# First two transfers moved ahead of the register moves, and SyncE's wait on the store moved into the closing block, in a streaming sum of absolute differences

## The chip, the cores and the metric

One core of one Trainium2 chip. Times are device microseconds of one execution of the program; the kernel before ran at 86.15 us (median of 6 runs beside the changed kernel). All runs told of here were in the fast state with a granted clock of 1.0. Profiles give a span, from the program's first record to its last; the time is 1.78 us longer than the span in nearly all runs (one exception is told below). Lines of the profile name VectorE DVE, ScalarE ACT, GpSimd POOL and SyncE SP; a q after the name means the engine's sequencer.

## The reference

```python
def reference(x, y, axis):          # x, y: 1024 x 4096 float32, axis -1
    return np.sum(np.abs(x - y), axis=axis).astype(np.float32)
```

33.55 MB go in, 4 KB come out.

## The kernel before

Rows lie on the 128 partitions, eight to each. SP loads x and the last four rows of y; ACT loads the first four rows of y. DVE subtracts, ACT takes the absolute value and sums along the row, the last row goes in four pieces that get smaller, and SP stores the eight sums of each partition. All waits are written by hand. The helper `put` takes an instruction just emitted and moves it into the program's first block: either ahead of the engine's opening drain, which is the start of the barrier that opens the program, or ahead of its branch out of that block.

```python
    def put(self, emit, early=False):
        ...
        before = "Drain" if early else "UnconditionalBranch"
        while len(here) > n:
            mine = here.pop(n)
            first = next(i for i, x in enumerate(main) if x.engine == mine.engine and x.opcode == before)
            main.insert(first, mine)
```

```python
    put(lambda: nc.sync.dma_start(out=xa, in_=xr[:, 0:H, :]).then_inc(s_first, 16), early=True)
    put(lambda: nc.scalar.dma_start(out=yb, in_=yr[:, 0:H, :]).then_inc(s_first, 16), early=True)
    put(lambda: nc.sync.dma_start(out=xb[:, 0:H - 1, :], in_=xr[:, H:K - 1, :]).then_inc(s_xb, 16))
    # ... (other loads, subtractions, sums)
    put(lambda: nc.sync.wait_ge(s_end, n_part + 3))
    put(lambda: nc.sync.dma_start(out=orr, in_=ro).then_inc(s_out, 16))
    put(lambda: nc.sync.wait_ge(s_out, 16))
```

The last line waits until the sums are in HBM. Behind it comes the closing block, which the framework writes: a barrier of all engines, GpSimd clearing the semaphores, a second barrier.

## Time and profile before

| | us |
|---|---|
| time, median (range) of 6 runs | 86.15 (85.93 to 86.25) |
| span of the profiled run | 84.33 |
| first issue to first data packet | 1.00 |
| first packet to last load's landing | 79.63 |
| last landing to the store's issue | 1.36 |
| store's issue to its landing | 1.41 |
| store's landing to the end | 0.93 |

The five rows below the span add up to it. The second of them is a stream at 421 GB/s and holds 94% of the span. The change moves no byte, so its effect is to be looked for in the other four, 4.7 us in all. The profile's lines for this are in the prediction below.

### The profile page before, as it was taken

How to read it: one execution, taken by the hardware profiler on the slowest of the kernel's cores; microseconds unless marked ns; L12 is line 12 of the kernel's file. 1: busy time of each engine (PE TensorE's matmuls, PEld its weight loads, DVE VectorE, ACT ScalarE, POOL GpSimd, SP SyncE). 2: the span in 40 equal slices, each digit the busy share in tenths (PEclk: the TensorE clock that was granted, in tenths of full speed). 3: DMA queues.
4: the chain of work that ended last, by engine and by line, in shares of the span. 5: the costliest groups of instructions: out<-in, count | busy, mean ns of one | idle time of the engine just before them, and what ended most of it. 6: DMA issues, size and time to landing. Idle time of an engine off the chain costs nothing.

```text
span 84.3 us, 98 instructions
## 1 busy us (share of the span) xinstructions
DVE 36.5 (43%) x15; ACT 31.2 (37%) x25; POOL 0.2 (0%) x4
## 2 busy tenths in 40 slices
DVE  0000000000000000000399999999199897988870
ACT  5000000000000000000002979797970967999950
POOL 0000000000000000000000000000000000000000
DMA  9199999983999999749999888899999999999900
GB/s 497 62 435 497 497 497 497 497 373 155 466 497 497 497 497 497 342 187 466 396 606 490 373 373 373 381 427 427 420 443 412 451 404 414 425 397 404 341 0 2
DMA packets 2160, 33.56 MB, mean 398 GB/s; under 512 B 368, under 2 KB 624, under 8 KB 1392
## 3 DMA queue, kind: packets, MB, share of 16 engines
q1 hardware_dynamic: 2016, 25.17, 70.9%
q10 hardware_dynamic: 144, 8.39, 23.0%
HBM read 33.55 MB, written 0.00 MB: 398 GB/s over the span
## 4 chain that ended last, share of the span: by engine, by line
DMA 67%; DVE 16%; ACT 13%; ACTq 1%; issue 0%
DMA yb_rows<-in_y_dram 67%; ACT xb_rows L110 13%; DVE xa_rows L105 10%; DVE xb_rows L105 5%; ACTq L176 1%; DVE ro_sums L140 1%
## 5 line engine op out<-in xcount | busy, mean ns | idle before, releaser
L105 DVE TENSOR_TENSOR xa_rows<-xa_rows,yb_rows 128x4096 f32<-128x4096 f32 x4 | 17.4, 4421 | 41.5 <-DMA yb_rows<-in_y_dram 41.5
L110 ACT ACTIVATE xa_rows<-xa_rows 128x4096 f32<-128x4096 f32 x4 | 14.5, 3617 | 45.6 <-DVE xa_rows L105 45.6
L105 DVE TENSOR_TENSOR xb_rows<-xb_rows,yb_rows 128x4096 f32<-128x4096 f32 (+5 forms) x8 | 17.8, 2241 | 3.5 <-DMA yb_rows<-in_y_dram 3.4
L110 ACT ACTIVATE xb_rows<-xb_rows 128x4096 f32<-128x4096 f32 (+5 forms) x8 | 14.9, 1859 | 3.7 <-DVE xb_rows L105 3.7
L110 ACT ACT_TABLE_LOAD x1 | 1.3, 1283 | 0.9 <-PEq L162 0.9
L110 ACT ACTIVATION_READ_ACCUMULATOR xb_rows<-xb_rows 128x1 f32 x8 | 1.5, 188 | 0.0
L110 ACT ACTIVATION_READ_ACCUMULATOR xa_rows<-xa_rows 128x1 f32 x4 | 0.7, 186 | 0.0
L140 DVE TENSOR_REDUCE ro_sums<-last_piece 128x1 f32<-128x387 f32 x1 | 0.6, 556 | 0.2 <-ACT xb_rows L110 0.2
L138 DVE TENSOR_TENSOR last_piece<-xb_rows,yb_rows 128x384 f32<-128x384 f32 x1 | 0.6, 557 | 0.2 <-DMA yb_rows<-in_y_dram 0.2
L132 DVE TENSOR_REDUCE ro_sums<-part_sums 128x1 f32<-128x3 f32 x1 | 0.2, 156 | 0.2 <-ACT xb_rows L110 0.2
L162 POOL MEMSET const-bfloat16-1.0<- 128x1 bf16 x1 | 0.1, 102 | 0.0
L162 POOL MEMSET const-uint8-127<- 128x1 uint8 x1 | 0.1, 102 | 0.0
L162 POOL MEMSET const-float32-0.0<- 128x1 f32 x1 | 0.1, 99 | 0.2 <-issue 0.2
L162 POOL MEMSET const-float32-1.0<- 128x1 f32 x1 | 0.1, 99 | 0.0
## 6 DMA issues: line engine op xcount, KB each, us to landing
xb_rows<-in_x_dram SPq DMA_DIRECT2D x1, 6144.0 KB, 54.9
yb_rows<-in_y_dram SPq DMA_DIRECT2D x3, 2048.0 KB, 15.3
xb_rows<-in_x_dram SPq DMA_DIRECT2D x1, 992.0 KB, 17.9
yb_rows<-in_y_dram SPq DMA_DIRECT2D x1, 992.0 KB, 16.4
xb_rows<-in_x_dram SPq DMA_DIRECT2D x1, 544.0 KB, 17.4
yb_rows<-in_y_dram SPq DMA_DIRECT2D x1, 544.0 KB, 18.2
xb_rows<-in_x_dram SPq DMA_DIRECT2D x1, 320.0 KB, 18.6
yb_rows<-in_y_dram SPq DMA_DIRECT2D x1, 320.0 KB, 18.9
```

Source lines behind the costliest of these rows:

```text
L105: put(lambda: nc.vector.tensor_sub(out=tx, in0=tx, in1=ty).then_inc(s_sub, 1))
L110: put(lambda: nc.scalar.activation(tx, tx, ABS, accum_out=to).then_inc(sem, 1))
L132: put(lambda: nc.vector.reduce_sum(out=ro[:, K - 2:K - 1], in_=part6, axis=AX).then_inc(s_end, 1))
L138: put(lambda: nc.vector.tensor_sub(out=last[:, n_part:n_part + w], in0=tx, in1=ty).then_inc(s_end, 1))
L140: put(lambda: nc.vector.reduce_sum(out=ro[:, K - 1:K], in_=last, axis=AX, apply_absolute_value=True).then_inc(s_end, 1))
L162: nc = _bacc.Bacc("TRN2", target_bir_lowering=False, num_devices=1)
L176: with _tile.TileContext(nc) as tc:
```

## The change

Its intent: put the first x and y issues still earlier, ahead of the register moves that the framework puts at the head of each engine's program; and let SP wait for the store not in the branch that leads to the closing block, but behind it, at the block's head.

```diff
-    def put(self, emit, early=False):
+    def put(self, emit, before="UnconditionalBranch"):
 ...
-        before = "Drain" if early else "UnconditionalBranch"
 ...
+    def at_end(self, emit):
 ...
+        def closing(ins):
+            if done or nc.cur_bb.bb.name == here or ins.engine != mybir.EngineType.SP:
+                return
+            done.append(ins)
+            emit()
 ...
-    put(lambda: nc.sync.dma_start(out=xa, ...).then_inc(s_first, 16), early=True)
-    put(lambda: nc.scalar.dma_start(out=yb, ...).then_inc(s_first, 16), early=True)
+    put(lambda: nc.sync.dma_start(out=xa, ...).then_inc(s_first, 16), before="RegisterMove")
+    put(lambda: nc.scalar.dma_start(out=yb, ...).then_inc(s_first, 16), before="RegisterMove")
 ...
-    put(lambda: nc.sync.wait_ge(s_out, 16))
+    entry.at_end(lambda: nc.sync.wait_ge(s_out, 16))
```

`closing` is called for each instruction ahead of its being added; at SP's first one in the closing block it emits the wait, which so comes to stand in front of it. When the program is finished, a wait that stands alone is folded into the instruction behind it, where it can be: in the kernel before into SP's branch, in the changed one into SP's first closing drain.

More of the change, by code (lines that the diff above doesn't have):

```diff
@@ L44, in put @@
             main.insert(first, mine)
+    def at_end(self, emit):
+        nc = self.nc
+        hook = nc.inst_callbacks[-1]
+        here = nc.cur_bb.bb.name
+        done = []
+        def closing(ins):
[3 more added lines that the diff above has]
+            emit()
+        nc.remove_inst_callback(hook)
+        nc.push_inst_callback(closing)
+        nc.push_inst_callback(hook)
 @with_exitstack
@@ L59 @@
     H = K // 2
-    put = Entry(nc).put
+    entry = Entry(nc)
+    put = entry.put
     def sbuf(name, shape):
@@ L81 @@
     s_out = tc.alloc_semaphore("s_out")
-    put(lambda: nc.sync.dma_start(out=xa, in_=xr[:, 0:H, :]).then_inc(s_first, 16), early=True)
-    put(lambda: nc.scalar.dma_start(out=yb, in_=yr[:, 0:H, :]).then_inc(s_first, 16), early=True)
+    put(lambda: nc.sync.dma_start(out=xa, in_=xr[:, 0:H, :]).then_inc(s_first, 16), before="RegisterMove")
+    put(lambda: nc.scalar.dma_start(out=yb, in_=yr[:, 0:H, :]).then_inc(s_first, 16), before="RegisterMove")
     put(lambda: nc.sync.dma_start(out=xb[:, 0:H - 1, :], in_=xr[:, H:K - 1, :]).then_inc(s_xb, 16))
```

## The prediction

> **What bounds the kernel now.** I read the page of the profile first, then the listing of the first and the last microseconds in order of time, then the records of the two lines that hold the program's opening (L162) and closing (L176), then SyncE's own waits.
>
> From the page:
>
> ```profile
> span 84.3 us, 98 instructions
> DVE 36.5 (43%) x15; ACT 31.2 (37%) x25; POOL 0.2 (0%) x4
> DMA  9199999983999999749999888899999999999900
> HBM read 33.55 MB, written 0.00 MB: 398 GB/s over the span
> DMA 67%; DVE 16%; ACT 13%; ACTq 1%; issue 0%
> ```
>
> The DMA row is at 7 or more in all but three of its first 38 slices of 2.1 us, and a low digit has a neighbour that makes up for it (packets of 64 KB are counted where they start). DVE and ACT are under half busy. The kernel is a stream of 33.55 MB from HBM: the trace's first data packet starts at 1.00 us and the last load lands at 80.63 us, so 33.55 MB / 79.63 us = 421 GB/s. That stretch is 79.6 of 84.3 us; neither part of the change touches a byte of it. What can be moved is the 1.0 us ahead of it and the 3.7 us behind it.
>
> The opening, in order of time (start, duration):
>
> ```profile
> 0.00 0.38 SPq L84 DMA_DIRECT2D xa_rows<-in_x_dram  x1
> 0.12 0.36 ACTq L85 DMA_DIRECT2D yb_rows<-in_y_dram  x1
> ...
> 0.91 1.28 ACT L110 ACT_TABLE_LOAD   x1 [0.91 <-PEq L162]
> 0.91 0.33 SPq L86 DMA_DIRECT2D xb_rows<-in_x_dram  x1
> ```
>
> The span starts with SP's issue of x: there is no earlier record of the program on any engine. The listing of L162, which holds whatever the program does before the kernel's own lines, shows what SP and ACT do besides:
>
> ```profile
> L162 DVEq DRAIN  x1: 10/10/10, 0.1 to 0.1; - x1
> ...
> L162 SPq DRAIN  x1: 131/131/131, 0.4 to 0.4; - x1
> L162 ACTq DRAIN  x1: 145/145/145, 0.5 to 0.5; - x1
> ...
> L162 SPq EVENT_SEMAPHORE  x1: 17/17/17, 0.8 to 0.8; - x1
> L162 ACTq EVENT_SEMAPHORE  x1: 17/17/17, 0.8 to 0.8; - x1
> ```
>
> The reader is to see what is missing: one drain and one semaphore wait each, and no register move. The source creates five on each engine (a zero and four bounds), but nothing reads them; in the finished program of this kernel, which I built and listed, they have been dropped, and the x issue is already SP's first instruction and the y issue ACT's.
>
> The end, in order of time, then the records of L176 and SP's own waits:
>
> ```profile
> 80.66 0.56 DVE L138 TENSOR_TENSOR last_piece<-xb_rows,yb_rows 128x384 f32<-128x384 f32 x1 [0.15 <-DMA yb_rows<-in_y_dram]
> 81.41 0.56 DVE L140 TENSOR_REDUCE ro_sums<-last_piece 128x1 f32<-128x387 f32 x1 [0.19 <-ACT xb_rows L110]
> 81.99 0.35 SPq L144 DMA_DIRECT2D out_dram<-ro_sums  x1
> ```
>
> ```profile
> L176 SPq DRAIN  x3: 7/7/7, 83.6 to 83.9; - x3
> L176 SPq COMPARE_BRANCH  x1: 32/32/32, 83.4 to 83.4; - x1
> ```
>
> ```profile
> SPq L176 <- DMA out_dram<-ro_sums: 1.1, 1, 1.1
> SPq L176 <- PEq L176: 0.6, 2, 0.4
> ```
>
> The last load lands at 80.63; subtraction and reduction end at 81.96; the store is issued at 81.99 and has landed at 83.40 (1.4 us from issue to landing on the page of issues). SP waits for it, and the instruction that waits is its branch into the closing block: the wait has been folded into it, so it is recorded as COMPARE_BRANCH. No other engine has a branch record on L176. Then two all-engine barriers run, and the last record ends at 84.33. The trace's own records, finer than the 0.1 us of this view, give SP's steps: store's last increment 83.396, COMPARE_BRANCH 83.413, DRAIN 83.564, DRAIN 83.629, GpSimd's collecting wait 83.662, release 83.740, SP released 83.782, second barrier until 84.33.
>
> **What the Trainium skill says.** "Advanced Engine Details and Errata", section Control Flow Timing, gives a compare-and-branch about 108 ns and an unconditional branch about 51 ns. The trace has 32 ns for the branch's own record, but 151 ns from its start to the start of the next instruction, where a drain takes 65 ns to the next one; I use the 151. "Perfetto Trace Analysis", section on the sequencer-only instruction, says that the recorded window opens when the semaphores are satisfied, so waiting is not in it. The trace agrees: the branch's record opens 17 ns after the store's last increment, though SP had been at it since 82.34. "VectorE: DVE Perf Modes", section "The DRAIN you can't avoid", tells boilerplate drains of about 12 ns from pipeline flushes; SP's closing drains are of that kind at 7 ns. "DMA: Bandwidth & Descriptors", section Latency and other measured facts, has about 600 ns to the first byte of a transfer issued from SP or ACT: here SP's first issue ends at 0.38 and the first packet starts at 1.00, which is 0.62 us. That is latency of the transfer itself and no reordering of SP's instructions shortens it.
>
> **The change part by part.**
>
> *The first two issues ahead of the register moves.* It takes five register moves per engine from in front of SP's and ACT's first issues. In the finished program there are none in front: 0 moves x anything = 0. The DRAIN and barrier after the issues stay. Gain 0.00 us at the front. If putting the transfers first made moves survive behind them, SP would run at most six small instructions between the issue and its first drain. From the 65 ns between two closing drains I estimate 6 x 65 ns = 0.4 us of delay for the opening barrier, so the second x issue would go from 0.91 to 1.3 us. That lies beside the first 16.8 MB, whose landing DVE awaits until 41.45 us; the queues don't run dry before then. ACT's table load of 1.28 us has until 45.91 us. Cost on the path: 0.00 us.
>
> *The wait on the store at the head of the closing block.* The number of waits doesn't change: the last increment of the store still lets SP go. What changes is which instruction wakes. Before: wake in COMPARE_BRANCH, 151 ns to the first drain, 65 ns to the second, 33 ns to the collecting wait. After: the branch waits for nothing and is done (or disappears, as on the other engines) at about 82.34 to 82.5, under the store's flight of 1.4 us. The wait then stands in front of SP's first closing drain, and I expect it to be folded into that drain as other waits have been folded into the instruction behind them. So: wake in the drain (17 ns after the increment, at 83.413), 65 ns to the second drain (83.478), 33 ns to the collecting wait (83.511 rather than 83.662). Saved: 83.564 - 83.413 = 0.151 us. If it is not folded, a semaphore wait by itself wakes first; SP's own one at 83.782 is followed by a drain at 83.873, 91 ns later, and the saving is 0.151 - 0.091 = 0.06 us. All this is on the path that sets the end: SP is the last of the engines at the first closing barrier (ACT's and DVE's drains end at 81.41 and 82.01), and the rest follows the collecting wait unchanged.
>
> Sum: 0.00 + 0.15 = 0.15 us, so the span goes from 84.33 to about 84.18. Time and span of the profiled run differ by 86.11 - 84.33 = 1.78 us, which neither part touches: 84.18 + 1.78 = 85.96. From the median of the runs, 86.2 - 0.15 = 86.05. I take 86.0 between them: -0.2%.
>
> **The rivals.**
>
> 1. *The moves are real and were in the way, unrecorded ahead of the span.* For it: measured time is 1.78 us longer than the span, so something runs outside the records. Against it: the drains and memsets of the same source line are recorded, moves aren't, and the finished program has none. If true, five moves at an estimated 65 ns would give 0.3 us more at the front, and the time about 85.7. It would show in the time, but not in the span.
> 2. *The wait that replaces the branch costs as much.* A drain with a wait could be as slow to go on as the branch: the opening drains took 131 and 145 ns, against 7 at the close. For it: exactly those were behind a fresh DMA issue, and the new one follows the store's issue. Against: there they came right after the issue, here the store's 1.4 us lie between, and today's first closing drain is also behind that store and takes 7 ns. If true, nothing is saved: 86.15.
> 3. *An earlier start of the stream speeds up or disturbs the loads.* Only if the first issue moved at all; and at 421 GB/s throughout, a shift by a few tenths shifts the landings by no more.
>
> **Range and chances.** The three runs of the kernel before lie between 85.93 and 86.25, a spread of 0.32 us, twice the effect. The range of 85.75 to 86.3 holds the 0.06 to 0.15 us cases, the first rival's 85.7 nearly, and the run-to-run spread. Two per cent is 1.7 us: the whole stretch from the last landing to the end is 3.7 us, of which the change touches 0.15, so faster has 0.01, slower 0.01, within 2% 0.98.
>
> **What would show it.** Right: first records unchanged (x issue at 0.00, y at 0.12, second x at 0.91, first drain of SP behind the x issue); no COMPARE_BRANCH on SP; a drain within 20 ns of the store's last increment, the second 65 ns later; from the store's last increment to the end 0.93 us before, 0.78 after. Wrong in the first part: move records, or a second x issue later than 0.91. Wrong in the second: a gap of 0.1 us or more between wake and second drain. The whole would be wrong if the time fell by over 0.4 us, or if the stretch up to the last landing moved by more than the runs' own spread.

## The result, and the profile after

86.01 us (median of 6 runs, 85.85 to 86.10) against 86.15; ratio 0.9986, 95% interval 0.9969 to 1.0003. A ratio is the mean time of one kernel's fast runs over that of the other's fast runs of the same rounds, so not quite the ratio of the medians. By itself this interval doesn't exclude 1; a second, longer measurement on another occasion (22 runs against 26) gave 0.9979, from 0.9970 to 0.9989:

> The changed kernel itself once more, beside the next run on the same chip, because its first ratio (0.9986, interval 0.9969 to 1.0003) rests on six executions and doesn't exclude 1. My theory (0.155 us shorter closing): ratio 0.998, interval clear of 1. Rival (no gain in the time, only in the records): 1.000.

So the change gains some two thousandths, and that is clear of the spread: the means differ by 0.18 us here and by 0.15 us in 22 further runs of the same finished program (the second part alone, below); in the first six runs it was 0.12 us. For the 2% question it is the same time.

Where it comes from is in the records. The same lines of the page as before, then the opening in order of time (start, duration):

```profile
span 84.1 us, 97 instructions
DVE 36.5 (43%) x15; ACT 31.2 (37%) x25; POOL 0.2 (0%) x4
...
HBM read 33.55 MB, written 0.00 MB: 399 GB/s over the span
...
DMA 67%; DVE 16%; ACT 13%; ACTq 1%; issue 0%
```

```profile
0.00 0.38 SPq L101 DMA_DIRECT2D xa_rows<-in_x_dram  x1
0.12 0.36 ACTq L102 DMA_DIRECT2D yb_rows<-in_y_dram  x1
...
0.91 1.28 ACT L127 ACT_TABLE_LOAD   x1 [0.91 <-PEq L179]
0.91 0.33 SPq L103 DMA_DIRECT2D xb_rows<-in_x_dram  x1
```

Busy times, bytes and the shares of the chain that ended last stand still. The opening is what it was, to the hundredth of a microsecond; 97 records instead of 98. The missing one shows in the listing of the closing line (L193 here, L176 before; name, count, duration in ns min/median/max, start of the first and of the last in us):

```profile
L193 SPq DRAIN  x3: 7/7/7, 83.4 to 83.7; - x3
```

and in SP's own waits:

```profile
SPq L193 <- DMA out_dram<-ro_sums: 1.1, 1, 1.1
SPq L193 <- PEq L193: 0.6, 2, 0.4
```

There is no COMPARE_BRANCH on SP any more, and the first of SP's three closing drains starts at 83.4 where it started at 83.6. The waits are the same two, as long as before: 1.1 us for the store, 0.6 us in the barriers. What was taken out lay between them. The trace's records to the nanosecond, in us of each span:

| | before | after |
|---|---|---|
| last load landed | 80.633 | 80.587 |
| store's last increment | 83.396 | 83.347 |
| SP wakes, in | 83.413 COMPARE_BRANCH | 83.364 DRAIN |
| SP's next drain | 83.564 | none between |
| SP's barrier drain | 83.629 | 83.425 |
| GpSimd's collecting wait | 83.662 | 83.457 |
| GpSimd's drain ahead of the clearing | 83.821 | 83.616 |
| end | 84.329 | 84.125 |
| from the store's last increment to the end | 0.933 | 0.778 |

The closing is 0.155 us shorter. The spans differ by 0.204 us; the other 0.049 us had been gained by the time the store landed, of which 0.046 at the last load. No part of the change reaches there, and one of the runs below, whose program is that of the kernel before, has its last load at 80.747: this is spread of the stream.

### The profile page after: what moved, and what is told of

It reads as the page before. It is cut to its first block, busy times and chain, and to the rows that moved or that the text cites. A ratio compares the mean times of both kernels' runs of the same rounds, so it can differ in the third digit from the quotient of the medians.

```text
span 84.1 us, 97 instructions
## 1 busy us (share of the span) xinstructions
DVE 36.5 (43%) x15; ACT 31.2 (37%) x25; POOL 0.2 (0%) x4
## 4 chain that ended last, share of the span: by engine, by line
DMA 67%; DVE 16%; ACT 13%; ACTq 1%; issue 0%
DMA yb_rows<-in_y_dram 67%; ACT xb_rows L127 13%; DVE xa_rows L122 10%; DVE xb_rows L122 5%; ACTq L193 1%; DVE ro_sums L157 1%
```

## The experiments

My theory: the first part changes nothing in the finished program, and the second gains by taking one instruction, the branch with its wait, out of the path from the store's landing to the barrier. The rivals: the moves do run, unseen, ahead of the span; or the gain hangs only on the branch being out of the way and not on which instruction carries the wait; or there is no gain but spread.

**The first part alone.** Before it ran I compared the two finished programs, engine by engine and instruction by instruction with all operands and waits (names and line numbers aside): 22 instructions on SP, 21 on ACT, 23 on DVE, 17 on GpSimd, 7 on TensorE, all the same as in the kernel before. So this run is also a measure of what two measurements of one program differ by.

```diff
-    entry.at_end(lambda: nc.sync.wait_ge(s_out, 16))      # from the changed kernel
+    put(lambda: nc.sync.wait_ge(s_out, 16))
```

> Only the first part of the change: the first x and y issues are put ahead of the register moves; the wait on the store stays in SP's branch. The finished programs of this kernel and of the kernel before are the same on all five engines, instruction by instruction. My theory (the moves are dropped when the program is finished, so the part is empty): ratio 1.000 within 0.002, no move in the records, second x issue at 0.91 us, 0.93 us from the store's last increment to the end, a COMPARE_BRANCH of 32 ns on SP. Rival (the moves run ahead of the span, unrecorded): some 0.3 us less in the time at an unchanged span, ratio 0.9965.

Ratio 0.9997 (0.9986 to 1.0007; 22 runs against 51). SP's COMPARE_BRANCH is back, and 0.934 us pass from the store's last increment to the end. The listing of its closing line:

```profile
L193 SPq COMPARE_BRANCH  x1: 33/33/33, 83.5 to 83.5; - x1
```

The rival's 0.9965 is outside the interval. The part is empty.

**The second part alone.** Its finished program is in turn the same as that of the whole change.

```diff
-    ... .then_inc(s_first, 16), before="RegisterMove")    # both first issues
+    ... .then_inc(s_first, 16), before="Drain")
```

> Only the second part: SP's wait on the store at the head of the closing block, the first issues where they were. My theory (all of the gain is the branch's 151 ns becoming a drain's 61 to 65 ns and a drain less of distance): 0.78 us from the store's last increment to the end, no COMPARE_BRANCH, ratio about 0.998 (0.15 of 86.1 us). Rival (the gain came with the first part, or was no gain but spread): 0.93 us or ratio 1.000.

Ratio 0.9979 (0.9969 to 0.9989; 22 runs against 51), 0.778 us from last increment to end. All of the gain is here.

**A wait that stands alone.** A second wait, on sums that were ready long before, takes the place in the first drain, so that the wait on the store stays an instruction by itself:

```diff
-    entry.at_end(lambda: nc.sync.wait_ge(s_out, 16))
+    def twice():
+        nc.sync.wait_ge(s_end, n_part + 3)
+        nc.sync.wait_ge(s_out, 16)
+
+    entry.at_end(twice)
```

> The changed kernel with a second, long satisfied wait (on the sums) at the head of the closing block, so that the wait on the store stays an instruction by itself and the drain behind it carries the other. My theory (the saving hangs on the wait being folded into the first drain; a wait that stands alone is followed by its drain 91 ns later): SP wakes in an EVENT_SEMAPHORE, 91 ns to the first drain, 61 to the second, so 0.87 us from the store's last increment to the end, ratio about 0.999. Rival (what saves is only that the branch is out of the way, whatever carries the wait): 0.78 us.

SP wakes in an EVENT_SEMAPHORE (the record of a semaphore wait that stands alone) at 83.550, drains at 83.610 and 83.675: 60 ns and 65 ns, and 0.842 us from last increment (83.533) to end (84.375). The wait's record, and SP's waits in this stretch:

```profile
L164 SPq EVENT_SEMAPHORE  x1: 17/17/17, 83.5 to 83.5; - x1
```

```profile
SPq L164 <- DMA out_dram<-ro_sums: 1.1, 1, 1.1
SPq L197 <- PEq L197: 0.6, 2, 0.4
```

So the instruction that carries the wait matters, as my theory has it: 0.842 lies between 0.778 (folded) and 0.933 (branch). But the size I gave it, 91 ns, was too large: 60 ns. I had read it off SP's wait in the barrier. That one also counts its semaphore down, and the drain behind it waits for the same semaphore to be zero; which of the two makes it longer no run shows. The time says nothing here: ratio 0.9994 (0.9973 to 1.0014; 14 runs against 51).

**The wait given to GpSimd.** If the closing is a chain, what stands in it matters only behind the store's landing. SP's wait puts the whole first barrier behind it. But the store need only have landed when GpSimd clears the semaphores; so GpSimd waits, behind the first barrier, and the barrier runs while the store is in flight. (The cut leaves out `at_end`'s edit: it now takes the engine and which of its drains in the closing block.)

```diff
-    entry.at_end(lambda: nc.sync.wait_ge(s_out, 16))
+    entry.at_end(lambda: nc.gpsimd.wait_ge(s_out, 16), mybir.EngineType.Pool, 1)   # at GpSimd's second drain there
```

> The wait on the store is taken from SP altogether and given to GpSimd, folded into its drain ahead of the clearing of the semaphores, behind the first closing barrier. SP arrives at that barrier while the store is still in flight. My theory (the whole first closing barrier, 83.41 to 83.82 in the kernel before, is on the path only because SP waits ahead of it): GpSimd's drain ends the wait 17 ns after the store's last increment, then 0.51 us as before from that drain to the end: 0.53 us from last increment to end, 0.40 us less than before and 0.25 less than the change, ratio about 0.995 to before. Rival (the closing barriers cost the same wherever the wait stands, or the store lands later when the engines run on): 0.78 us or more, ratio 0.998.

Ratio 0.9934 (0.9913 to 0.9955; 6 runs), median 85.64 us. To read it, first GpSimd's records on the closing line of the kernel before, then those of this one:

```profile
L176 POOLq EVENT_SEMAPHORE  x4: 17/17/17, 83.7 to 84.2; - x4
L176 POOLq EVENT_SEMAPHORE_RANGE_CLEAR  x1: 113/113/113, 83.9 to 83.9; - x1
```

```profile
L196 POOLq EVENT_SEMAPHORE  x4: 17/17/17, 82.5 to 83.8; - x4
L196 SPq DRAIN  x3: 7/7/123, 82.3 to 82.7; - x3
L196 POOLq EVENT_SEMAPHORE_RANGE_CLEAR  x1: 113/113/113, 83.5 to 83.5; - x1
```

GpSimd's first collecting wait is now at 82.5, 0.8 us ahead of the store's landing (83.324), where it was 0.27 us behind it. GpSimd's drain, which carries the wait, starts at 83.348, and the end is at 83.856: 0.532 us from last increment to end, 0.40 less than before. SP waits no longer for the store:

```profile
SPq L196 <- PEq L196: 1.2, 2, 1.1
```

Its first drain took 123 ns instead of 7: it now comes 56 ns behind the end of the store's issue. That is hidden too. The run was repeated, because 0.9934 is more than 0.40 us explain:

> The kernel with GpSimd waiting for the store once more; its first ratio, 0.9934 from six executions, is 0.002 below what the 0.40 us of its trace explain (0.9953). My theory (only the closing shrinks): 0.9953, interval including it, 0.53 us from last increment to end, store 1.41 us from issue to landing. Rival (something more is gained that the closing doesn't show): 0.9934 again.

0.9943 (0.9922 to 0.9963; 6 runs against 26), median 85.66 us, 0.533 us from last increment to end and 1.419 us for the store. The interval holds the 0.9953 of the theory, and so did the first. Both means are some 0.5 us below that of before, though, 0.1 us more than the closing shows. In the two traces the rest lies ahead of the store, where this edit doesn't reach: the last load lands at 80.569 and 80.496, 0.064 and 0.137 us earlier than in the trace of before. With 6 runs each I leave open whether that is spread. This kernel beats both: correct, and 0.3 us under the changed one (means of 85.67 and 85.98 us on the same occasion).

**What a part at the front would have been worth.** The first part was empty; whether the front is on the path at all is another question. Drains stay in the finished program, so they can stand where the moves would have stood. All three kernels of this set have the changed closing.

```diff
+    for _ in range(24):
+        put(lambda: nc.sync.drain(), before="RegisterMove")
+    for _ in range(24):
+        put(lambda: nc.scalar.drain(), before="RegisterMove")
     put(lambda: nc.sync.dma_start(out=xa, ...
```

> The changed kernel with 24 drains ahead of the first issue on SP and on ACT: instructions that do stay in the program, where the dropped moves would have stood. Theory (what stands ahead of both first issues is on the path in full, so the first part of the change gained nothing only because there was nothing to pass): about 24 x 61 to 65 ns = 1.5 us later first packet, last load and end, ratio about 1.016 to before (1.5 less the 0.15 of the closing). Rival (a few instructions at the front are hidden by the transfers' latency of 0.6 us or by the stream): first packet at most 0.9 us later, ratio under 1.010.

Ratio 1.0098 (1.0084 to 1.0112; 4 runs against 41). The expected 1.5 us were wrong in size. The opening in order of time:

```profile
0.93 0.38 ACTq L106 DMA_DIRECT2D yb_rows<-in_y_dram  x1
1.25 0.36 SPq L105 DMA_DIRECT2D xa_rows<-in_x_dram  x1
```

24 drains cost SP 1.25 us, 52 ns each, and ACT 0.93 - 0.12 = 0.81 us, 33 to 34 ns each: less than the 61 to 65 ns between SP's closing drains. And the first data packet, at 1.941 us, is now y's: it follows the earlier of the two issues by 1.008 us. The number of the rival (under 1.010) came true, but not what it says: nothing was hidden by the latency, since issue to packet is 1.0 us as before, and the packet is 0.94 us later. The stream then takes 79.55 us, the last load lands at 81.491, and the closing is the changed kernel's 0.778. The time grew by a little more than the span; time less span is 1.95 us in this kernel instead of 1.78, and what makes up that 0.17 us no record shows. It stays open.

If the earlier issue counts, then delaying SP's alone must cost next to nothing:

```diff
+    for _ in range(24):
+        put(lambda: nc.sync.drain(), before="RegisterMove")
     put(lambda: nc.sync.dma_start(out=xa, ...
```

> The same 24 drains ahead of SP's first issue alone; ACT's y issue stays at the front. Theory (the stream is of both queues and only its first packet counts, since the first subtraction awaits both transfers): y's packets start at about 1.1 us in place of x's, the last load is 0.1 to 0.2 us later than without the drains, ratio about 1.000 to before. Rival (SP's queue has more than its share of the bytes, 25 of 33.6 MB, and its delay comes out at the end): 1.5 us later, ratio 1.016.

```profile
0.13 0.38 ACTq L104 DMA_DIRECT2D yb_rows<-in_y_dram  x1
1.25 0.37 SPq L103 DMA_DIRECT2D xa_rows<-in_x_dram  x1
2.02 1.28 ACT L129 ACT_TABLE_LOAD   x1 [2.02 <-PEq L181]
2.02 0.33 SPq L105 DMA_DIRECT2D xb_rows<-in_x_dram  x1
```

SP's first issue is 1.25 us late, yet the first packet (y's) comes at 1.146, 0.15 us later than before, and the last load lands at 80.779, 0.15 us later than before. The last load alone would prove little, since it came at 80.747 in a kernel without drains; but the ratio is 0.9996 (0.9989 to 1.0003; 21 runs against 41), which fits 0.15 us lost at the front and 0.155 gained at the close. The stream is one, whichever queue's packets begin it: 1.25 us of delay in one queue's start became 0.15 us. The second x issue, 1.1 us later than before, and ACT's table load, as late, cost nothing on top.

Last, six drains ahead of both, as many as the source has instructions there that are dropped (the five register moves and one more):

```diff
+    for _ in range(6):   # and the same for nc.scalar
+        put(lambda: nc.sync.drain(), before="RegisterMove")
```

> Six drains ahead of both first issues, the number of instructions that the source has ahead of SP's and of ACT's first issue and that are dropped from the finished program. Theory: 6 x 61 to 65 ns = 0.37 to 0.39 us later first packet and end; against the kernel before 0.38 - 0.15 = 0.23 us more, ratio about 1.0025. So much the first part would have been worth. Rival: under the spread, ratio 0.998 as the change itself.

```profile
0.32 0.38 SPq L105 DMA_DIRECT2D xa_rows<-in_x_dram  x1
0.34 0.39 ACTq L106 DMA_DIRECT2D yb_rows<-in_y_dram  x1
```

SP's issue moved by 0.317 us, the first packet from 0.999 to 1.321, the ratio is 1.0015 (1.0009 to 1.0022; 21 runs against 41). The expected 1.0025 lies outside the interval: it was worked out with 61 to 65 ns a drain, and here they cost 52. From 0.32 us at the front less 0.155 at the close I get 0.17 us, or 1.0019, which lies inside. So the front is on the path one for one, within the interval, and passing six instructions of a drain's kind would have been worth 0.32 us, twice what the second part gained. There was nothing to pass.

Over all of these kernels the stretch from the first packet to the last load's landing is 79.5 to 79.8 us, whichever queue began it.

## Why the prediction was right

It was right in the time (86.0 predicted, 86.01 measured), and the steps that carry it were:

- *First two issues: 0.00 us.* Right, and for the reason given: the finished programs are the same (first run), and the opening's records stood still in the changed kernel.
- *Wait in the closing block: 0.151 us.* Right: 0.155 in the records, 0.778 us from last increment to end where 0.78 was named. The wait was folded into the first drain, SP woke 17 ns after the increment, and the collecting wait came 32 ns behind the second drain. The one difference is 61 instead of 65 ns between the two drains.
- *The unfolded case: 0.06 us saved.* The mechanism was right, the size wrong: 60 ns for the wait that stands alone, not 91, so 0.09 us saved.
- *First rival, moves that run unseen.* Refuted by the identical program and by 0.9997. Its 65 ns for an instruction at the head, an estimate from closing drains, was too large: drains there cost 52 ns on SP and 33 to 34 on ACT.
- *Second rival, a drain with a wait as slow as the branch.* Refuted by 61 ns. Its ground was good all the same: a drain right behind an issue takes 123 to 153 ns in each of these traces where one stands there (131 and 145 at the opening, 123 behind the store where GpSimd waits); the changed kernel escapes it because its drain waits 1.1 us for the store first.
- *Third rival, a stream that starts earlier disturbs.* It had no occasion; the runs with drains moved its start by up to 0.94 us and its length by no more than its spread.
- The range was wide for the effect. It had to be: with six runs each, the spread of 0.3 us is twice the gain, and only 22 runs against 26 put the interval clear of 1. It holds the unchanged 86.15 too, so the time alone would have passed a change that does nothing; what bears the prediction out is its list of records. And that 86.0 came within 0.01 us of the median is luck: it was set between two sums 0.09 us apart, and the six runs spread over 0.25 us. The span fell by 0.204 us and not by 0.15, and the surplus is the 0.049 us of the stream's spread.

## What to carry to other kernels

Look at the finished program before reordering its source: an instruction that isn't in it can't be passed. Records that are missing from the first microsecond of a trace hint at this but don't prove it, for the branches that carry no wait are in these programs and left no record either. In this kernel, bound by its stream, the first issue and the chain behind the store's landing counted one for one; in one like it, ask of each instruction behind the landing whether it needs the landing at all. That question, put to the whole barrier and not to one branch, gave 0.40 us in the records where the change gave 0.155.

## What the Trainium skill lacked or had wrong

- "Advanced Engine Details and Errata", Control Flow Timing: a compare-and-branch is given as about 108 ns, an unconditional branch as about 51 ns, and a branch that carries a wait isn't told of. Here one that SP had waited in, into the next block, took 151 ns from its start to the next instruction's, and taking it out of the chain saved 155 ns; its own record shows 32 ns. The trace calls it COMPARE_BRANCH, but in the program it is SP's unconditional branch with the wait folded in (`put` inserts ahead of `UnconditionalBranch`), so the 151 ns don't refute the page's 108; why it takes longer than the 60 ns of a wait that stands alone is open. Unconditional branches without a wait left no record in these traces. From the end of the store's issue to the drain behind such a branch it is 56 ns; at the opening 48 ns lie between an issue and a drain with no branch between. The difference of 8 ns leaves little room for the page's 51 ns, unless the branch runs beside the issue, which no record shows.
- "VectorE: DVE Perf Modes", The DRAIN you can't avoid: boilerplate drains are told as a constant 12 ns or so. Here SP's drains and ACT's took 7 to 14 ns where their engine had no work left, but 123 to 153 ns where they came within 60 ns of the end of a transfer's issue on the same engine.
- No page that I read has what a drain costs from start to start: 52 ns on SP and 33 to 34 ns on ACT where it stands in a row at the head of the program, 61 to 65 ns on SP in the closing block.
